# The low parts of gate and up's operands, of sixteen weight units and of products 5 and 7: GpSimd's share of the subtractions given to VectorE

## The chip, the cores and the metric

The kernel runs on one core of a Trainium2 chip. The metric is the device time of one execution in microseconds (us). The engines have queues of their own: TensorE (PE; its weight loads are PEld) does the matrix products, VectorE (DVE) and GpSimd (POOL) element-wise work, ScalarE (ACT) copies, casts and functions, and SyncE (SP) issues the transfers.

## The reference

A decoder of two layers on 1024 tokens of width 1024, in float32. A layer normalises its input and makes one input projection whose columns go to three token mixers, an RWKV-7 recurrence, a dilated window attention and a latent attention. Their outputs are joined, projected and added to the input. Then comes the part that the change touches:

```python
    for l in range(DEPTH):
        ...
        x = x + jnp.concatenate([ya, yb, yc], axis=-1) @ w_out[l]
        h = rms_norm(x, ffn_norm_g[l])
        x = x + (jax.nn.silu(h @ ffn_w_gate[l]) * (h @ ffn_w_up[l])) @ ffn_w_down[l]
    return rms_norm(x, final_norm_g)
```

`D_FF` is 2816, that is 22 columns of 128 in `ffn_w_gate` and `ffn_w_up`.

## The kernel before

All matrices are held as tiles of 128x512, with features on the partitions and half of the tokens (512) along the row. A product of two float32 matrices is made from three matmuls: each operand is split into a high part, its cast to the matmul's type, and a low part, the rest, and `mm3` sums high by high, high by low and low by high in PSUM. A split is one cast on ScalarE (`acopy`, L295, rows named `wh`, `hhi`, `mhi`, `ahi`) and one subtraction of 128x512 on VectorE or GpSimd (`tt`, L301, rows named `wl`, `hlo`, `mlo`, `alo`). Which of the two it is, `split` is told by its caller.

Gate and up are made with Strassen's scheme: the matrix of 8 by 2 blocks of activations and a pair of weight columns give seven products of four blocks each (twelve matmuls) in place of eight. Product 1 takes the weight block a11, 6 takes a21+a22-a11, 7 takes a11-a21, 2 takes a12, 5 takes a21+a22, 4 takes a22 and 3 what is left; the right operands are sums of `hx`, the normalised activations, made by `sums` on VectorE. They are made in the order 1, 6, 7, 2, 5, 4, 3. There are eleven pairs for each of gate and up, so 22 blocks (`Four`) in a layer. Of the first eight of them products 1 and 2 come ahead of all others (`early`), since these need only the first half of the tokens: their sixteen operands are the weight units `("g"...)` and `("u"...)` of `loader`, while all later weight operands are made by `Operands`. A `Four` uses four banks of PSUM. ScalarE copies product 1 out (`u`), and then product 2 may be added to its bank; VectorE adds product 6 to `u`, product 7 to that (`v<-u,gu`), after which product 4 may use 7's bank, and product 5 (`v<-v,gu`), after which product 3 may use 5's. The results of gate and up are multiplied on GpSimd (`v<-v`; one of four on VectorE), VectorE makes the sums that the down product needs from them, splits these seven (`alo`), and they go to DRAM. Down's first eighteen rows of blocks are made by the same scheme from `Operands` in three stages of four blocks each, the last four rows in the plain way.

The order of every engine's queue is fixed when the program is built. Strands of work (generators) are run by a planner (`Flow.run`): it keeps a clock for each engine, prices an operation (`tt`: columns x 1.04 + 65 ns on VectorE, x 2.2 + 65 ns on GpSimd, `F.op`), and takes next the strand that can start first, with a lower `prio` number first among those that could start at the same time. Strands of weights and of adds out of PSUM have 2, operand sums and the splits of activations mostly 3. Nothing is reordered at run time: an instruction at the head of its engine's queue holds up what is behind it. The weights go through a ring of six operand pairs, so that a further one is split only after an earlier one was used.

The operand splits of gate and up (`put`) and those of the mixers' outputs (`mix_split`) ask `sub_eng` for their engine, which names VectorE and GpSimd by turns. The weight units are split on GpSimd; of the products' operands 6, 2 and 4 are split on VectorE, 1, 3, 5 and 7 on GpSimd.

Of the kernel before, what the change touches and what calls it, by code (L numbers as in the profile page):

```python
# [231 lines left out]
def trunk(ctx: ExitStack, tc: tile.TileContext, xT, pos, vec, con, first, w_in, small, uq, uqr, ukv,  # L232
# [60 lines left out]
    def acopy(out, in_):  # L293
        F.op("act", cols(in_) * 0.833 + 80)
        nc.scalar.copy(out=out, in_=in_)  # L295
# [3 lines left out]
    def tt(eng, out, a, b, op):  # L299
        F.op(eng, cols(out) * (1.04 if eng == "dve" else 2.2) + 65)  # L300
        ENG[eng].tensor_tensor(out=out, in0=a, in1=b, op=op)  # L301
# [22 lines left out]
    def dma(out, in_, nbytes):  # L324

        s = F.cur
        start = max(s.at(), F.clock["dma"])
        F.clock["dma"] = start + max(450.0, nbytes / 360.0)
        nc.sync.dma_start(out=out, in_=in_)
        return F.clock["dma"] + 2000  # L330
# [8 lines left out]
    def f32(ap):  # L339
        return ap.bitcast(F32)  # L340
# [22 lines left out]
    def room(level):  # L363

        return lambda: sum(max(n, 0) for lv, n in reserve.items() if lv < level)

    def pages(where, names, dt=F32, keep=0, of=None):

        def taken(n):
            if of in reserve:  # L370
                reserve[of] -= n

        got = yield Need(lambda: [P[w] for w in where], len(names), keep, taken if of else None)
        of = of if of in reserve else None
        out = []
        for n, s in zip(names, got):
            n, d = n if isinstance(n, tuple) else (n, dt)
            t = s.pool.tile([128, HALF], d, tag="hp", name=n)
            owner[id(t)] = (s, t, of)
            out.append(t)  # L380
        return out

    def page(where, name, dt=F32, keep=0, of=None):
        return (yield from pages(where, [name], dt, keep, of))[0]

    def free(*tiles):
        for t in tiles:
            s, _, of = owner.pop(id(t))
            if of is few:
                F.give(few)  # L390
            elif of in reserve:
                reserve[of] += 1
            F.give(s)
# [68 lines left out]
    def sub_eng():  # L462
        flip[0] ^= 1
        return "dve" if flip[0] else "pool"

    def split(src, hi, lo, eng):

        yield "act"
        acopy(hi, src)
        yield eng  # L470
        tt(eng, lo, src, f32(hi), ALU.subtract)
# [5 lines left out]
    def again(k):  # L477
        return k[0] in pairs_dram and k[2] == 1
# [3 lines left out]
    def loader(items):  # L482

        there.update({k: Event() for k, _ in items if k[0] in pairs_dram})

        def keep(k):
            late, soon = room(4), room(1)
            at = k[1][0][1] if k[0] == "S" else k[1]
            return lambda: soon() if k[0] == "in" or at < at_layer[0] else late()

        def own(k):

            rest, ffn = keep(k), k[0] in "gusS"
            return lambda: room(3.2)() if ffn and 3.2 in reserve else rest()

        def parts(k, srcs):

            if k[0] != "S":
                return [(Event(), srcs)]
            n = range(len(k[1]))  # L500
            at = [(g, 0) for g in n] + [(g, b) for g in n for b in (1, 2)] + [(g, 3) for g in n]
            return [(Event(), srcs[g][b], g, b) for g, b in at]

        def pair(k):

            return pairs_dram[k[0]][k[1], k[3], k[4]]

        queue = [(k, [] if again(k) else parts(k, srcs), own(k)) for k, srcs in items]

        def fetch():  # L510
            for k, todo, keep in queue:
                for ev, part, *_ in todo:
                    yield Need([raws])
                    wr = yield from page(["gp"], "wr", keep=keep, of=3.2)
                    w, t = 0, 0.0
                    yield "dma"
                    for a in part:
                        n = a.shape[-1]
                        t = dma(wr[:, w:w + n], a, 512 * n)
                        w += n  # L520
                    F.set(ev, wr, t)

        def raw_free(wr):
            free(wr)
            F.give(raws)

        F.spawn(fetch(), 1)
        for k, todo, keep in queue:
            if again(k):
                yield there[(*k[:2], 0, *k[3:])]  # L530
                yield Need([ring])
                w = yield from pages(["gp"], ["wh", "wl"], F32R, keep, 3.2)
                at = pair(k)
                yield "dma"
                for i in range(2):
                    t = dma(f32(w[i]), at[i], 262144)
                F.set(W[k], w, t)
                continue
            if k[0] == "S":
                gs = []  # L540
                for g, key in enumerate(k[1]):
                    evs = {b: ev for ev, _, g_, b in todo if g_ == g}
                    gs.append(Operands(key, k[2], evs, todo[0][1][0].shape[-1], keep, raw_free))
                for r in k[2]:
                    for g in gs:
                        yield from g.make(r)
                continue
            wr = yield todo[0][0]
            yield Need([ring])
            wh, wl = yield from pages(["gp"], ["wh", "wl"], F32R, keep, 3.2)  # L550
            yield from split(wr, wh, wl, "pool")
            raw_free(wr)
            now = F.cur.at()
            if k[0] in pairs_dram:
                yield "dma"
                for i, w in enumerate((wh, wl)):
                    t = dma(pair(k)[i], f32(w), 262144)
                F.set(there[k], None, t)
            F.set(W[k], (wh, wl), now)

    class Operands:
# [6 lines left out]
        def out(self, r, src, then=None):  # L568
            yield Need([ring])
            wh, wl = yield from pages(["gp"], ["wh", "wl"], F32R, self.keep, 3.2)  # L570
            w = self.w

            def one():
                yield from split(src[:, w], wh[:, w], wl[:, w], "dve" if r in (6, 2, 4) else "pool")
                if then:
                    then(src)
                F.set(W[(*self.key, r)], (wh, wl))

            F.spawn(one(), 2)
# [433 lines left out]
    def layer(l):  # L1013
# [1058 lines left out]
        def ffn():  # L2072
# [50 lines left out]

            def put(src, ev, where_=both, last=True):
                hi, lo = yield from pages(where_, ["hhi", "hlo"], F32R, keep)
                yield from split(src, hi, lo, sub_eng())
                if last:
                    free(src)
                F.set(ev, (hi, lo))

            def first_half(k):
                a = yield hx[0][k]
                F.spawn(put(a, Bg[1][k], last=False), 3)
                a = yield hx[0][k + 4]
                F.spawn(put(a, Bg[2][k], last=False), 3)

            def sums(k):
                b12 = yield hx[1][k]
                b22 = yield hx[1][k + 4]
                b11, b21 = hx[0][k].val, hx[0][k + 4].val  # L2140
                t1, t2 = yield from pages(both, ["t1", "t2"], keep=keep)
                yield "dve"
                tt("dve", t1, b12, b11, ALU.subtract)
                yield "dve"
                tt("dve", t2, b22, t1, ALU.subtract)
                F.spawn(put(t2, Bg[6][k], last=False), 2)
                yield "dve"
                tt("dve", b12, b22, b12, ALU.subtract)
                F.spawn(put(b12, Bg[7][k]), 2)
                F.spawn(put(t1, Bg[5][k]), 3)  # L2150
                yield Bg[1][k]
                free(b11)
                yield Bg[2][k]
                yield "dve"
                tt("dve", b21, b21, t2, ALU.subtract)
                F.spawn(put(b21, Bg[4][k]), 3)
                F.spawn(put(b22, Bg[3][k]), 3)
                yield Bg[6][k]
                free(t2)
# [5 lines left out]
            for hf in range(2):  # L2165
# [4 lines left out]
                for c in range(KD):  # L2170
# [4 lines left out]
                    for n_, k in enumerate(KORDER):  # L2175
# [4 lines left out]
                        w = yield W["wo", l, hf, c, k // 4]  # L2180
# [354 lines left out]
        def weights():  # L2535
            yield w_start
            yield from loader(items)
# [24 lines left out]
    def first_weights():  # L2562
        F.cur.t = 1500.0
        yield from loader(in_items(0))
# [139 lines left out]
```

## Time and profile before

| what | value |
|---|---|
| median of 3 runs | 2620.64 us (2617.64 to 2624.98) |
| the profiled execution's own time | 2621.2 us |
| its span, first to last instruction | 2619.4 us |
| TensorE busy | 2533.5 us, 97% |
| VectorE busy | 1747.4 us, 67% |
| ScalarE busy | 1135.3 us, 43% |
| GpSimd busy | 1154.9 us, 44% |
| mean granted TensorE clock | 0.983 |

Times in the profile are counted from the first instruction. Gate and up begin at about 655 us in layer 0 and at about 1949 us in layer 1. A busy share is an average over stages that differ; what TensorE waits for has to be read stage by stage.

### The profile page before, as it was taken

How to read it: one execution, taken by the hardware profiler on the slowest of the kernel's cores; microseconds unless marked ns; L12 is line 12 of the kernel's file. 1: busy time of each engine (PE TensorE's matmuls, PEld its weight loads, DVE VectorE, ACT ScalarE, POOL GpSimd, SP SyncE). 2: the span in 40 equal slices, each digit the busy share in tenths (PEclk: the TensorE clock that was granted, in tenths of full speed). 3: DMA queues.
4: the chain of work that ended last, by engine and by line, in shares of the span. 5: the costliest groups of instructions: out<-in, count | busy, mean ns of one | idle time of the engine just before them, and what ended most of it. 6: DMA issues, size and time to landing. Idle time of an engine off the chain costs nothing. (4 is left out here: it accounts for less than half of the span.)

```text
span 2619.4 us, 38866 instructions
## 1 busy us (share of the span) xinstructions
PE 2533.5 (97%) x13112; PEld 2030.1 (78%) x13112; DVE 1747.4 (67%) x3415; ACT 1135.3 (43%) x2313; POOL 1154.9 (44%) x914
## 2 busy tenths in 40 slices
PE   7899999999899999999999999999998999999998
PEld 6678765888688888888878787568887888888887
DVE  6856677764987657566567376677458877665566
ACT  6542475663434334323354326557544334333221
POOL 3513231366645444455553123214655544444660
PEclk9999998999999999999999999999999999999999
DMA  7662321135255434896485241201461545449851
GB/s 265 234 211 88 118 64 29 56 115 199 99 176 194 140 134 161 307 316 229 166 290 194 93 171 36 63 25 53 168 198 60 197 165 177 147 136 351 291 196 65
DMA packets 235800, 417.55 MB, mean 159 GB/s; under 512 B 27600, under 2 KB 45264, under 8 KB 235472
## 3 DMA queue, kind: packets, MB, share of 16 engines
q1 hardware_dynamic: 235600, 415.07, 46.6%
q8 instruction: 103, 1.69, 0.3%
q14 instruction: 97, 0.79, 0.1%
HBM read 269.60 MB, written 141.69 MB: 157 GB/s over the span
## 5 line engine op out<-in xcount | busy, mean ns | idle before, releaser
L301 POOL TENSOR_TENSOR wl<-wr,wh 128x512 fp32r<-128x512 f32 (+1 forms) x304 | 436.5, 1448 | 387.0 <-ACT wh L295 310.2
L266 PE MATMUL gu<-hhi,wh 128*128 128x512 f32 x1232 | 483.7, 393 | 22.8 <-ACT u L295 16.5
L266 PE MATMUL gu<-hlo,wh 128*128 128x512 f32 x1232 | 481.1, 390 | 0.0
L266 PE MATMUL gu<-hhi,wl 128*128 128x512 f32 x1232 | 481.0, 390 | 0.0
L266 PEld LDWEIGHTS gu<-hhi,wh 128*128 128x128 f32 x1232 | 232.3, 189 | 79.6 <-ACT u L295 18.1
L295 ACT CAST wh<-wr 128x512 fp32r<-128x512 f32 (+1 forms) x424 | 244.4, 593 | 77.3 <-POOL wl L301 21.4
L266 PEld LDWEIGHTS gu<-hhi,wl 128*128 128x128 f32 x1232 | 232.3, 189 | 48.6
L266 PEld LDWEIGHTS gu<-hlo,wh 128*128 128x128 f32 x1232 | 232.4, 189 | 47.7
L301 POOL TENSOR_TENSOR wl<-s,wh 128x512 fp32r<-128x512 f32 (+1 forms) x136 | 181.5, 1342 | 197.1 <-ACT wh L295 142.8
L266 PE MATMUL dn<-bhi,wh 128*128 128x512 f32 (+1 forms) x664 | 252.0, 380 | 0.0
L266 PE MATMUL dn<-blo,wh 128*128 128x512 f32 (+1 forms) x664 | 251.5, 379 | 0.0
L266 PE MATMUL dn<-bhi,wl 128*128 128x512 f32 (+1 forms) x664 | 251.2, 379 | 0.0
L266 PE MATMUL inp<-hhi,wh 128*128 128x512 f32 x512 | 213.9, 418 | 11.4 <-ACT wh L295 11.4
L295 ACT CAST wh<-s 128x512 fp32r<-128x512 f32 (+1 forms) x204 | 116.8, 581 | 247.0 <-DVE s L301 199.7
L266 PE MATMUL inp<-hhi,wl 128*128 128x512 f32 x512 | 205.6, 401 | 5.2 <-POOL wl L301 5.2
L266 PE MATMUL inp<-hlo,wh 128*128 128x512 f32 x512 | 204.9, 400 | 1.2 <-DVE hlo L310 1.2
L301 DVE TENSOR_TENSOR x<-x,dn 128x512 f32<-128x512 f32 (+1 forms) x160 | 104.6, 657 | 109.3 <-PE dn L266 86.7
L301 DVE TENSOR_TENSOR v<-u,gu 128x512 f32<-128x512 f32 x132 | 90.1, 682 | 126.4 <-PE gu L266 126.2
L301 POOL TENSOR_TENSOR v<-v 128x512 f32<-128x512 f32 x66 | 98.0, 1488 | 134.3 <-DVE v L301 133.4
L291 ACT ACTIVATE P<-P,mx 128x512 f32<-128x512 f32 (+1 forms) x192 | 117.5, 613 | 63.9 <-DVE mx L857 42.5
L266 PEld LDWEIGHTS dn<-bhi,wh 128*128 128x128 f32 x664 | 124.9, 188 | 23.5
L266 PEld LDWEIGHTS dn<-bhi,wl 128*128 128x128 f32 x664 | 124.9, 188 | 23.4
(319 smaller groups left out, 5403.6 us busy)
## 6 DMA issues: line engine op xcount, KB each, us to landing
act_dram<-ahi SPq DMA_DIRECT2D x142, 256.0 KB
act_dram<-alo SPq DMA_DIRECT2D x142, 256.0 KB
bhi<-act_dram SPq DMA_DIRECT2D x142, 256.0 KB
blo<-act_dram SPq DMA_DIRECT2D x142, 256.0 KB
wr<-in_w_gate_dram SPq DMA_DIRECT2D x104, 256.0 KB
wr<-in_w_up_dram SPq DMA_DIRECT2D x104, 256.0 KB
wr<-in_w_in_dram SPq DMA_DIRECT2D x72, 256.0 KB
pairs_in<-wh SPq DMA_DIRECT2D x72, 256.0 KB
```

The source lines that it names most:

```text
L266: nc.tensor.matmul(out=out, lhsT=lhsT, rhs=rhs, start=start, stop=stop, **kw)
L291: nc.scalar.activation(out=out, in_=in_, func=func, **kw)
L295: nc.scalar.copy(out=out, in_=in_)
L301: ENG[eng].tensor_tensor(out=out, in0=a, in1=b, op=op)
```

## The change

Three places in which the low part was made by GpSimd, wholly or by turns, name VectorE: the sixteen weight units of gate and up, the weight operands of products 5 and 7 (of gate, up and down), and all operands of gate and up. Weight units of the input and output projections and of the last part of down, and products 1 and 3, stay on GpSimd. `sub_eng` isn't called by `put` any more, so `mix_split` and the norms have its turns to themselves.

```diff
@@ loader @@
             wh, wl = yield from pages(["gp"], ["wh", "wl"], F32R, keep, 3.2)
-            yield from split(wr, wh, wl, "pool")
+            yield from split(wr, wh, wl, "dve" if k[0] in "gu" else "pool")
             raw_free(wr)
@@ Operands.out @@
             def one():
-                yield from split(src[:, w], wh[:, w], wl[:, w], "dve" if r in (6, 2, 4) else "pool")
+                yield from split(src[:, w], wh[:, w], wl[:, w], "dve" if r in (6, 2, 4, 5, 7) else "pool")
                 if then:
@@ ffn, put @@
                 hi, lo = yield from pages(where_, ["hhi", "hlo"], F32R, keep)
-                yield from split(src, hi, lo, sub_eng())
+                yield from split(src, hi, lo, "dve")
                 if last:
```

## Rows read from the trace of the kernel before

**Rows 1.** The page, span and part 1: busy us, share of the span, instructions.

```profile
span 2619.4 us, 38866 instructions
...
PE 2533.5 (97%) x13112; PEld 2030.1 (78%) x13112; DVE 1747.4 (67%) x3415; ACT 1135.3 (43%) x2313; POOL 1154.9 (44%) x914
```

**Rows 2.** Windows: length, busy us (instructions) of PE, PEld, DVE, ACT, POOL; clock, DMA.

```profile
655.00:720.50 65.50, 55.33 (x243) 44.92 (x242) 59.82 (x67) 31.14 (x55) 41.60 (x27) 0.95 0.30 98
...
1179.00:1244.50 65.50, 65.50 (x290) 54.26 (x289) 43.30 (x64) 20.65 (x44) 38.66 (x32) 1.00 0.68 229
```

**Rows 3.** TensorE's waits over the span: us in total, times, longest.

```profile
PE gu L266 <- ACT u L295: 16.5, 4, 6.0
...
PE gu L266 <- DVE v L301: 3.2, 12, 1.3
PE gu L266 <- ACT ahi L295: 3.1, 4, 0.9
```

**Rows 4.** TensorE's timeline, three places: start, us, instruction, [idle before, releaser].

```profile
686.04 0.39 PE L266 MATMUL gu<-hhi,wl 128*128 128x512 f32 x1
688.72 0.50 PE L266 MATMUL gu<-hhi,wh 128*128 128x512 f32 x1 [2.29 <-ACT u L295]
...
699.52 0.39 PE L266 MATMUL gu<-hhi,wl 128*128 128x512 f32 x1
705.87 0.80 PE L266 MATMUL gu<-hhi,wh 128*128 128x512 f32 x1 [5.96 <-ACT u L295]
...
1999.63 0.79 PE L266 MATMUL gu<-hhi,wh 128*128 128x512 f32 x1 [5.93 <-ACT u L295]
```

**Rows 5.** Windows around the long wait, columns as in rows 2 (clock third from last).

```profile
692.00:700.00 8.00, 7.91 (x35) 6.20 (x34) 8.00 (x7) 4.93 (x9) 8.00 (x5) 1.00 0.31 98
...
706.00:712.00 6.00, 6.00 (x21) 4.85 (x22) 5.41 (x6) 2.97 (x6) 4.82 (x4) 0.77 0.14 50
...
2000.00:2006.00 6.00, 6.00 (x15) 4.62 (x15) 5.45 (x6) 2.41 (x6) 4.36 (x3) 0.52 0.01 5
```

**Rows 6.** Timelines of VectorE, GpSimd and ScalarE, 655 to 715 us.

```profile
665.36 5.36 DVE L310 SCALAR_TENSOR_TENSOR hx<-x,vecs,ssum 128x512 f32<-128x512 f32 x8 [0.74 <-PE ssum L276]
...
695.57 5.17 DVE L301 TENSOR_TENSOR hlo<-hx,hhi 128x512 fp32r<-128x512 f32 x3
...
704.00 0.68 DVE L301 TENSOR_TENSOR s<-s,wr 128x512 f32<-128x512 f32 x1
...
698.46 5.07 POOL L301 TENSOR_TENSOR hlo<-hx,hhi 128x512 fp32r<-128x512 f32 x3
...
686.44 1.22 ACT L295 CAST hhi<-hx 128x512 fp32r<-128x512 f32 x2 [1.62 <-DVE hx L301]
...
688.09 0.58 ACT L295 COPY u<-gu 128x512 f32<-128x512 f32 x1
...
704.71 0.62 ACT L295 CAST wh<-s 128x512 fp32r<-128x512 f32 x1 [5.01 <-DVE s L301]
705.24 0.58 ACT L295 COPY u<-gu 128x512 f32<-128x512 f32 x1
```

**Rows 7.** Windows of layer 0's start of gate and up, columns as in rows 2.

```profile
665.00:706.00 41.00, 32.75 (x145) 26.50 (x143) 40.55 (x40) 21.50 (x38) 26.15 (x16) 0.95 0.21 69
706.00:815.00 109.00, 107.45 (x464) 87.75 (x465) 92.18 (x118) 42.39 (x76) 52.59 (x35) 0.99 0.50 169
```

**Rows 8.** VectorE's waits in 665 to 706 us: all that there are.

```profile
DVE hx L310 <- PE ssum L276: 0.7, 1, 0.7
```

**Rows 9.** Timelines of VectorE, GpSimd and TensorE in the steady stage, around 914 us.

```profile
914.59 1.28 DVE L301 TENSOR_TENSOR alo<-v,ahi 128x512 fp32r<-128x512 f32 x2
...
917.00 0.68 DVE L301 TENSOR_TENSOR v<-v,gu 128x512 f32<-128x512 f32 x1
...
913.82 4.41 POOL L301 TENSOR_TENSOR wl<-wr,wh 128x512 fp32r<-128x512 f32 x1 [5.11 <-ACT wh L295]
...
917.82 0.47 PE L266 MATMUL gu<-hhi,wh 128*128 128x512 f32 x1 [0.17 <-DVE v L301]
```

## The prediction

> **What bounds the kernel now.** The page comes first: TensorE is busy for 2533.5 of 2619.4 us, VectorE for 1747.4, GpSimd for 1154.9 [rows 1]. A reader should take from it that a gain can come only from time in which TensorE doesn't get its next matmul, some 86 us, and that the question is how much of this the edited splits cause. The windows tell where it is. In a slice where nothing is late TensorE shows 65.50 of 65.50 us and 290 matmuls, 0.226 us each; in the slice in which gate and up begin it shows 55.33 and 243 [rows 2]. The list of TensorE's waits names what it waited for there: the copy `u` of ScalarE, 16.5 us in four waits over the whole span, so two in each layer, and in small pieces `v` of VectorE (3.2 us) and `ahi` (3.1 us) [rows 3]. TensorE's timeline gives the two long waits of layer 0: from 686.04 to 688.72, and from 699.52 to 705.87; the later one of layer 1 ends at 1999.63 and is as long [rows 4]. After it the granted clock falls as well: 0.77 in 706 to 712 us and 0.52 in 2000 to 2006, so part of both is at 1.2 GHz, while after the shorter wait it stays at 1.00 [rows 5].
>
> Why does `u` come late, a copy out of PSUM of 0.58 us? ScalarE's timeline shows it behind others in ScalarE's queue: the one at 688.09 stands behind casts of `hx` for which ScalarE waited 1.62 us, the one at 705.24 behind the cast of `s`, for which it waited 5.01 us, and that operand is a sum of VectorE made at 704.00 [rows 6]. So VectorE is late. In 665 to 706 it is busy 40.55 of 41 us with only 40 operations [rows 7], and all that it waited there is 0.7 us at the start [rows 8]. It works without a pause, and slowly: three rests `hlo` take 5.17 us, over 1.7 each, beside GpSimd's three at 1.7 each [rows 6]. Where VectorE runs through undisturbed, two rests take 1.28 us together and a single operation 0.68, so one follows another every 0.60 us [rows 9]. In this stretch the two engines take turns: one operation of each in about 1.72 us.
>
> **The change part by part.** Nothing is computed twice and nothing added: a subtraction of 128x512 goes from one queue to the other. Per layer there are 14 of the 28 operand rests (each second one so far), 16 weight units, and products 5 and 7 of 22 gate and up blocks and 12 down blocks, 68: together 98, so 196 in all. No DMA and no wait on a DMA queue is moved. What changes with it is order: the program's queues are written by a planner that prices a VectorE subtraction at about 0.60 us and a GpSimd one at 1.19, each as if the other engine weren't there. The first price is the undisturbed row of VectorE; what the contended rows cost isn't in it. With the rests on VectorE the planned queue should thus be nearer to the time that it really takes.
>
> *The start of gate and up.* GpSimd has 16 operations in 665 to 706, and VectorE 40 [rows 7]. All of these 16 are units or operand rests and move. VectorE then has 56. Eight are the normalised `hx`, which read PSUM and are no slower today (eight in 5.36 us [rows 6]); the other 48 at 0.60 make 28.8: 34.1 us in all, from 665.4 to 699.5. At 0.68 each, the isolated price, it would be 37.9 us, to 703.3. Today the same work ends at about 704.7 for the sum that matters.
>
> What TensorE can win there, in layer 0: the waits of 2.29 and 5.96 us, and 0.16 more for each, since a matmul's row is 0.39 long and the pitch 0.23: 8.57 us [rows 4]. The lower clock in 706 to 712 costs 6 x 0.23 = 1.4 us, in 2000 to 2006 6 x 0.48 = 2.9 us [rows 5]. Layer 1 repeats the waits, so both layers have 2 x 8.57 + 4.3 = 21.4 us.
>
> What may be left of it: without the first wait TensorE asks for the second `u` at 699.75 - 2.45 = 697.3. If the sum of `s` stays at the end of VectorE's 56 operations, `u` is done at 699.5 + 1.1 (cast and copy) = 700.6, a rest of 3.3 us; by the isolated price at 704.4, 7.1 us, which is the whole wait again. If the planner brings this sum forward (sums of weights go ahead of the operand sums in its ranking) nothing is left. I take 1.5 us for each layer, nearer to the lower end, since the row with two back to back gives 0.60 and not 0.68: 21.4 - 3.0 = 18.4 us. A wait of that size left the clock at 1.00 [rows 5], so its part goes with the wait.
>
> *Steady gate and up.* In 706 to 815, where the first eight blocks make five products each, VectorE is busy 92.18 of 109 us in 118 operations, 0.78 each, and GpSimd has 35 [rows 7]. Some 17 of those move: 17 x 0.60 = 10 us more for VectorE, against contention of (0.78 - 0.65) x 118 = 15 us over 35 operations, 0.44 each, so 7.5 us less. VectorE ends at some 95 of 109 us: fuller, not full. The cover is this room of 14 us; where it lacks, see the second rival. I take nothing, with both ends kept: the small waits for `v` and `ahi` all gone would be 6.3 us of idle and some 2.5 of pitch, 9 us; the loss is the second rival's.
>
> *Down.* TensorE was at 65.50 of 65.50 beside 43.30 of VectorE in such a slice [rows 2]; twelve blocks bring two rests each, 24 x 0.60 = 14 us spread over some 200 us per layer. Nothing: it lies behind matmuls that don't wait.
>
> The sum: 2621.2 us is the profiled execution's own time, 1.8 more than its span and 0.6 above the median of 2620.64. 2621.2 - 18.4 = 2602.8, which against the median is 2602.
>
> **A rule and its row.** At 913.82 a GpSimd rest took 4.41 us while VectorE went on at 0.60 [rows 9]: there GpSimd paid for the overlap and VectorE nothing. The Trainium skill (SBUF — State Buffer, "Who interferes with whom") says that a VectorE instruction with two SBUF inputs and a GpSimd instruction that reads SBUF exclude each other for the whole instruction, and that the order of issue decides who is blocked. The trace agrees with that second half by the 4.41 us, and with exclusion by the 1.7 us. This speaks against the change wherever VectorE runs without a pause, since a rest on GpSimd is then free for VectorE and costs it 0.60 after the move. By the row of 1.7 us the steady stage costs nothing and the sum stays 2602; by this rule alone each moved rest in a burst is a loss, and the sum is that of the second rival.
>
> **The rivals.** First, VectorE's one queue bounds the start: 3.3 to 7.1 us of the second wait stay in each layer. For it: VectorE is already full there, and the operations grow from 40 to 56. Against: 56 at 0.60 are fewer microseconds than 40 contended ones. The gain is then 21.4 - 6.6 = 14.8 at best and, with the whole wait and the clock's fall back, 2 x 2.45 = 4.9 us: between 2606 and 2616, about 2613.
>
> Second, it gets slower by one mechanism: product 3 takes over the bank of product 5 and can start only when VectorE has added that into `v`. At 917.00 this add stands behind a run of rests of activations, and the matmul after it waits 0.17 us [rows 9]: no room is left. Each block boundary between up and the next gate has such a burst, 11 a layer. A moved rest of product 5 or 7 that is put in front of that add delays product 3 by its 0.60 us in full. One a burst: 22 x 0.60 = 13 us; two: 26 us, 2602 + 26 = 2628; two in every one of the 44 blocks, 53 us, 2655. It decides from two a burst on. Against it: the planner ranks that add above the rests of activations, so that a moved rest should push one of those back, not the add; and a GpSimd rest that now holds VectorE up in the burst, at the 0.44 us worked out above, goes with the move.
>
> Third, the move does what it says and the planner's new order gives the time back: each later choice, layer 1's attention too, is made from other clocks, and a chain of small operations can come out some microseconds longer. The price is that of the gain: 2621 within 8 us. For it speaks that the order is decided at build time over the whole span; against it, that the operations of those other stages don't change and that nothing in the profile gives their shift a direction. That rests go to GpSimd again by another path is excluded: the diff names all three.
>
> **How the numbers follow.** The forecast has 0.60, 2593 to 2612, with 2602 in it. The first rival 0.15, about 2613, of which 0.06 is faster by over 0.3% (7.9 us, below 2612.8) and 0.09 not; 0.3% is also about what a measurement here tells from no change. The second 0.15, 0.11 beyond 2628 and 0.04 with one rest a burst, near 2615 to 2620. The third 0.10: 0.07 within, 0.01 faster, 0.02 slower. Faster 0.67, same 0.20, slower 0.13. The range goes from 2593 (18.4 us and the 9 us of small waits) to 2619, which takes in the first rival and leaves out the second's worse half.
>
> **What would show it.** After the change there should be no GpSimd rest at all between the start of gate and up and its first product 3, VectorE's operations there some 0.6 us apart with some 56 of them in 35 us, no wait of TensorE for `u` over 2 us, and a granted clock of 1.00 through that stretch in both layers. VectorE's busy time over the span should rise by less than 196 x 0.60 = 118 us, since contention goes. I am wrong if `u` still ends waits of 5 us (first rival), if waits for `v` of a microsecond come at each boundary (second), or if those waits are gone and others of the same sum stand elsewhere (third).

## The result and the profile after

The changed kernel takes 2596.07 us (2587.61 to 2599.44) against 2622.81 (2617.64 to 2625.68) in the runs of both: a ratio of 0.989, interval 0.9872 to 0.9909, that is 24 to 34 us. The forecast was 2602 and faster.

The page after the change, span and part 1, as in [rows 1]:

```profile
span 2597.7 us, 38718 instructions
...
PE 2536.6 (98%) x13112; PEld 2035.6 (78%) x13112; DVE 1785.0 (69%) x3611; ACT 1134.1 (44%) x2313; POOL 883.5 (34%) x718
```

VectorE has exactly the 196 operations more (3415 to 3611) and GpSimd 196 fewer. VectorE's busy time rose by 37.6 us only, 0.19 for each operation, while GpSimd's fell by 271. At 0.60 us each the moved operations alone would be 118 us, so something like 80 us of VectorE's busy time went elsewhere; the experiments show that it was time spent held up by GpSimd.

The windows of the changed kernel, columns as in [rows 2]: the 41 us from the first normalised operands on (it is the stretch of [rows 7], which lies 9 us later here), the stage of the early blocks, gate and up in both layers from first to last matmul, and what comes before them:

```profile
673.80:714.80 41.00, 41.00 (x184) 33.96 (x183) 40.35 (x66) 25.69 (x46) 3.05 (x1) 1.00 0.27 88
716.00:825.00 109.00, 108.56 (x479) 89.31 (x478) 91.66 (x138) 41.34 (x74) 32.63 (x21) 1.00 0.54 181
665.60:1090.00 424.40, 422.55 (x1862) 347.61 (x1861) 320.56 (x492) 170.09 (x309) 106.84 (x70) 1.00 0.50 169
1942.40:2366.90 424.50, 422.65 (x1863) 347.67 (x1862) 321.34 (x494) 170.12 (x309) 106.84 (x70) 1.00 0.49 170
...
0.00:571.60 571.60, 543.35 (x3261) 416.60 (x3262) 389.07 (x1018) 303.40 (x662) 193.91 (x189) 0.95 0.37 124
```

The same windows of the kernel before:

```profile
655.50:1094.50 439.00, 425.13 (x1863) 348.23 (x1862) 319.36 (x429) 170.86 (x310) 209.04 (x136) 0.99 0.48 164
1949.20:2388.70 439.50, 426.76 (x1863) 349.43 (x1862) 317.40 (x429) 171.17 (x310) 212.03 (x136) 0.99 0.48 164
...
0.00:561.50 561.50, 531.14 (x3262) 406.75 (x3262) 390.69 (x1018) 303.55 (x662) 193.08 (x189) 0.97 0.38 127
```

Gate and up take 14.6 us less in layer 0 and 15.0 less in layer 1, with 63 VectorE operations more in about the same busy time (319.36 and 320.56 us). The first stretch, before the output projection, has the same instructions on all engines in both kernels and took 10.1 us longer in this profiled execution, at a mean granted clock of 0.95 against 0.97. So the spans differ by only 21.7 us, and the profiled execution of the changed kernel is the slowest of its four. From here on stages are compared, not spans.

At the start VectorE is as full as before (40.35 of 41 us), but makes 66 operations in it where it made 40 [rows 7]: 0.61 each. TensorE is busy for 41.00 of 41.00 at a clock of 1.00. The one GpSimd operation there is a weight rest of product 3; the prediction wanted none before the first product 3, which can't be, since product 3's own weights are still split on GpSimd. TensorE's waits in gate and up of layer 0, first after and then before:

```profile
PE gu L266 <- DVE v L301: 1.4, 6, 0.2
PE gu L266 <- ACT ahi L295: 0.4, 1, 0.4
```

```profile
PE gu L266 <- ACT u L295: 8.2, 2, 6.0
PE gu L266 <- DVE v L301: 2.1, 6, 1.3
PE ssum L276 <- DVE ry L310: 1.9, 1, 1.9
PE gu L266 <- ACT ahi L295: 1.5, 2, 0.9
```

Both waits for `u` are gone, and so is one that the prediction had not counted: `ssum <- ry`, where TensorE waited for the last step of the norm's root.

### The profile page after: what moved, and what is told of

The parts are those of the page before. It is cut to its first block, busy times and chain, and to the rows that moved or that the text cites. A ratio compares the mean times of both kernels' runs of the same rounds, so it can differ in the third digit from the quotient of the medians.

```text
span 2597.7 us, 38718 instructions
## 1 busy us (share of the span) xinstructions
PE 2536.6 (98%) x13112; PEld 2035.6 (78%) x13112; DVE 1785.0 (69%) x3611; ACT 1134.1 (44%) x2313; POOL 883.5 (34%) x718
## 5 line engine op out<-in xcount | busy, mean ns | idle before, releaser
L301 POOL TENSOR_TENSOR wl<-wr,wh 128x512 fp32r<-128x512 f32 (+1 forms) x204 | 279.9, 1384 | 189.4 <-ACT wh L295 157.0
L301 POOL TENSOR_TENSOR wl<-s,wh 128x512 fp32r<-128x512 f32 (+1 forms) x68 | 94.3, 1395 | 452.9 <-ACT wh L295 371.7
L266 PE MATMUL inp<-hhi,wh 128*128 128x512 f32 x512 | 215.0, 420 | 10.1 <-ACT wh L295 10.1
L301 POOL TENSOR_TENSOR v<-v 128x512 f32<-128x512 f32 x66 | 105.7, 1602 | 208.6 <-DVE v L301 183.1
L301 DVE TENSOR_TENSOR wl<-wr,wh 128x512 fp32r<-128x512 f32 (+1 forms) x220 | 156.8, 717 | 18.3 <-ACT wh L295 17.9
L301 POOL TENSOR_TENSOR x<-x,u 128x512 f32<-128x512 f32 x72 | 103.9, 1473 | 153.6 <-DVE u L301 136.6
```

The lines of the kernel that those rows point to most:

```text
L266: nc.tensor.matmul(out=out, lhsT=lhsT, rhs=rhs, start=start, stop=stop, **kw)
```

## The experiments

Times are medians of 5 to 12 executions; the kernel before, run beside them, had medians of 2621.35, 2621.86 and 2623.26 us in the three sets.

**The three parts, each alone.** The diff's hunks one at a time. First the operands:

```diff
-                yield from split(src, hi, lo, sub_eng())
+                yield from split(src, hi, lo, "dve")
```

> Only the operand rests of gate and up go to VectorE (14 a layer); units and products 5 and 7 stay on GpSimd. Contention theory: 9 of GpSimd's 16 operations in the first 41 us of gate and up go, so about 9/16 of what that stretch gives back, some 25 us over both layers, is won: 14 us, near 2608; GpSimd still has its weight rests beside VectorE's operations of 1.7 us. Rival, that the planner's new order makes the gain: no relation to the share, anything from 2596 to 2625.

2610.09 us, ratio 0.9959 (0.9946 to 0.9972): near the 2608 of the contention theory, but within the rival's wide range too, so the time alone doesn't part them. Gate and up took 432.9 us in layer 0; of the long wait 1.1 us is left, and the norm's 1.9 us stay, since the weight units were still with GpSimd there:

```profile
PE gu L266 <- DVE v L301: 2.9, 7, 1.9
PE ssum L276 <- DVE ry L310: 1.9, 1, 1.9
...
PE gu L266 <- ACT u L295: 1.1, 1, 1.1
```

Then the weight units alone:

```diff
-            yield from split(wr, wh, wl, "pool")
+            yield from split(wr, wh, wl, "dve" if k[0] in "gu" else "pool")
```

> Only the sixteen weight units go to VectorE; operand rests by turns, products 5 and 7 on GpSimd. Contention theory: 7 of 16 operations go and with them the long tiny operations of the norm before it: about 11 + 4 us, near 2607. Rival (new order): no relation to the share, 2596 to 2625.

2634.71 us, ratio 1.0055 (1.0036 to 1.0074): slower, by 14 us, where the contention theory had forecast 14 faster. The forecast by shares fell. Gate and up took 445.7 us in layer 0 and 445.6 in layer 1, 6.7 and 6.1 more than before, so nearly all of the loss is there. TensorE's waits in layer 0 show two effects:

```profile
PE gu L266 <- DVE v L301: 8.0, 6, 1.3
PE gu L266 <- ACT u L295: 5.0, 2, 3.8
PE gu L266 <- ACT ahi L295: 4.0, 2, 3.2
```

The norm's wait is gone and those for `u` are shorter (5.0 for 8.2), as the theory wants. But the waits for `v` went from 2.1 to 8.0 us, six times 1.3, in the later part of gate and up, where no weight unit is left. (Those for `ahi` grew too, from 1.5 to 4.0; what made them longer wasn't traced.) A burst there, on VectorE, GpSimd and TensorE, shows what lengthens the waits for `v`:

```profile
924.30 2.38 DVE L301 TENSOR_TENSOR alo<-v,ahi 128x512 fp32r<-128x512 f32 x2
...
929.02 0.67 DVE L301 TENSOR_TENSOR v<-v,gu 128x512 f32<-128x512 f32 x1
...
924.19 1.35 POOL L301 TENSOR_TENSOR wl<-wr,wh 128x512 fp32r<-128x512 f32 x1 [4.57 <-ACT wh L295]
...
929.84 0.47 PE L266 MATMUL gu<-hhi,wh 128*128 128x512 f32 x1 [1.35 <-DVE v L301]
```

It is the burst of [rows 9] with one difference. There GpSimd's rest came while VectorE was running through and took 4.41 us, at no cost to VectorE. Here it starts at 924.19, 0.11 us ahead of the first `alo`, and takes 1.35; the two `alo` take 2.38 us in place of 1.28. VectorE is 1.1 us later at `v<-v,gu`, and TensorE's wait grew by 1.35 - 0.17 = 1.18. In the new plan the cast that this rest waits for stands one place earlier on ScalarE. The Trainium skill (SBUF — State Buffer, "Who interferes with whom") says that the order of issue decides which of the two is held up; these two bursts, 4.41 us on the one side and 1.1 on the other, agree that either can be. The 4.41 us are more than that order gives, which the prediction didn't say: GpSimd's row there begins at 913.82, and the two `alo` from 914.59 on, which begin later, went ahead of it all the same [rows 9]. No run here shows why.

Products 5 and 7 alone:

```diff
-                yield from split(src[:, w], wh[:, w], wl[:, w], "dve" if r in (6, 2, 4) else "pool")
+                yield from split(src[:, w], wh[:, w], wl[:, w], "dve" if r in (6, 2, 4, 5, 7) else "pool")
```

> Only products 5 and 7 of the weights go to VectorE. In the start of gate and up nothing of them runs, so both long waits for the copy u stay (2.3 and 6 us a layer). Contention theory: at most the small waits of later pairs go, 2 to 6 us, near 2618. The rival of the prediction by which bursts get longer: 13 us slower with one more rest a burst, near 2635. New order alone: within 2615 to 2625.

2619.48 us, ratio 0.9994 (0.9979 to 1.0009): no change, and no sign of the slower rival. The `u` waits stayed (9.3 us in layer 0, two). Together the three parts bring 27 us, singly 11, -14 and 1.6: they don't add up. Two reasons fit the traces, without being parted here: what each leaves on GpSimd goes on holding up VectorE, and each makes a plan of its own.

**Engines against order.** To part the two, the subtraction was priced on one engine's clock and issued on another. In the first cross everything is planned as before and the moved rests are issued on VectorE:

```diff
+        if plan:
+            yield plan
+            F.op(plan, cols(lo) * (1.04 if plan == "dve" else 2.2) + 65)
+            ENG[eng].tensor_tensor(out=lo, in0=src, in1=f32(hi), op=ALU.subtract)
+            return
...
-                yield from split(src, hi, lo, sub_eng())
+                yield from split(src, hi, lo, "dve", sub_eng())
```

> All three parts issued on VectorE, but planned at the price and on the clock of GpSimd as before, so that the order of TensorE, ScalarE and of everything that isn't moved is that of the kernel before. Contention theory: most of the gain comes without a new order, at least 20 of some 27 us, near 2600. Rival (new order makes the gain): the long waits for u stay, since u stands behind the same casts, and the time is 2615 to 2622.

2605.00 us, ratio 0.9936 (0.9919 to 0.9954): 17 us of the 27, less than the 20 that were expected, and well outside the rival's 2615 to 2622. The old order was kept nearly: by the traces three matmuls, two ScalarE instructions and some eight of VectorE's unmoved operations stand elsewhere in each layer. The start of gate and up lost its waits but for one of 1.2 us, and in the bursts those for `v` grew from 0.17 to 0.78. The window of gate and up in layer 0, and the waits in it:

```profile
660.30:1089.40 429.10, 423.14 (x1861) 347.17 (x1861) 323.49 (x495) 170.48 (x310) 103.91 (x70) 1.00 0.49 168
...
PE gu L266 <- DVE v L301: 4.7, 6, 0.8
PE gu L266 <- ACT wh L295: 1.2, 1, 1.2
```

The burst's rows, VectorE and TensorE, in this run (L473 is the line added to `split`, so a moved rest) and then in the changed kernel:

```profile
908.28 1.28 DVE L301 TENSOR_TENSOR alo<-v,ahi 128x512 fp32r<-128x512 f32 x2
909.49 0.68 DVE L473 TENSOR_TENSOR wl<-wr,wh 128x512 fp32r<-128x512 f32 x1
910.09 1.28 DVE L301 TENSOR_TENSOR alo<-t,ahi 128x512 fp32r<-128x512 f32 x2
911.29 0.68 DVE L301 TENSOR_TENSOR v<-v,gu 128x512 f32<-128x512 f32 x1
...
912.12 0.47 PE L266 MATMUL gu<-hhi,wh 128*128 128x512 f32 x1 [0.78 <-DVE v L301]
```

```profile
911.65 0.68 DVE L301 TENSOR_TENSOR wl<-wr,wh 128x512 fp32r<-128x512 f32 x1
912.25 0.68 DVE L301 TENSOR_TENSOR alo<-v,ahi 128x512 fp32r<-128x512 f32 x1
912.85 0.68 DVE L301 TENSOR_TENSOR alo<-t,ahi 128x512 fp32r<-128x512 f32 x1
913.45 0.68 DVE L301 TENSOR_TENSOR v<-v,gu 128x512 f32<-128x512 f32 x1
...
914.65 0.68 DVE L301 TENSOR_TENSOR alo<-t,ahi 128x512 fp32r<-128x512 f32 x1
...
914.28 0.47 PE L266 MATMUL gu<-hhi,wh 128*128 128x512 f32 x1 [0.25 <-DVE v L301]
```

One moved rest (`wl`, at 909.49) ahead of the add makes TensorE's wait 0.61 us longer: the second rival's mechanism at its price. In the changed kernel the rest stands there too, but the planner has put one `alo` behind the add for it, so the wait is 0.25.

The other cross has the changed kernel's plan, with the rests issued where they were before.

```diff
-                yield from split(src, hi, lo, sub_eng())
+                yield from split(src, hi, lo, sub_eng2(), "dve")
```

> The other cross: planned as the changed kernel, all moved rests priced on VectorE's clock, but issued on the engines of before (units and products 5 and 7 on GpSimd, operands by turns). Contention theory: VectorE is contended again, so the waits for u are back and the time is 2612 to 2630. Rival (new order makes the gain): 2596 to 2605.

2632.17 us, ratio 1.0035 (1.0019 to 1.0050). TensorE's matmuls stand exactly in the order of the changed kernel, and this order with the old engines is slower than the kernel before. The waits are back, but not where they were expected: those for `u` are 0.6 us, those for `v` 10.4. Layer 0:

```profile
663.20:1106.80 443.60, 427.88 (x1862) 350.40 (x1861) 318.43 (x429) 169.28 (x309) 195.31 (x136) 0.99 0.47 162
...
PE gu L266 <- DVE v L301: 10.4, 8, 5.5
...
PE gu L266 <- ACT u L295: 0.6, 1, 0.6
```

From the windows from first to last matmul of gate and up, layer 0, in us:

| | rests issued as before | rests issued on VectorE |
|---|---|---|
| planned as before | 439.0 | 429.1 |
| planned as changed | 443.6 | 424.4 |

In this layer the engines are worth 9.9 us with the old plan and 19.2 with the new; the plan is worth 4.7 us, and only with the new engines. Layer 1 gives 11.0, 19.1 and 4.0.

**Contention put back.** GpSimd makes each moved rest a second time into a tile that nothing reads, and the planner doesn't know of it. The tile needs the room of one page, so a run of the changed kernel with 78 pages stands beside it.

```diff
+    idle = fix.tile([128, HALF], F32, name="idle")
...
         tt(eng, lo, src, f32(hi), ALU.subtract)
+        if twin:
+            n = cols(lo)
+            nc.gpsimd.tensor_tensor(out=idle[:, :n], in0=src, in1=f32(hi), op=ALU.subtract)
```

> The changed kernel, and GpSimd makes each moved rest once more into a tile that nobody reads, unpriced by the planner, so that GpSimd's old work stands beside VectorE's new. One page fewer in the big pool (78), as in the run beside it. Contention theory: VectorE's operations at the start of gate and up take 1.7 us again, now 56 of them, and the time goes back to before or beyond it: 2620 to 2660. Rival (the gain lies in the order or in GpSimd's chain being off the path): nobody waits for the copies, so 2596 to 2602.

> The changed kernel with one page fewer in the big pool (78 for 79), the measure for the run with the doubled rests. All theories: as the changed kernel, 2590 to 2602.

With the copies 2652.69 us (ratio 1.0127, 1.0104 to 1.0149), without 2581.58 (0.9853, 0.9823 to 0.9883). Windows of gate and up in layer 0, first with the copies, with 63 us at the start and TensorE's longest waits, then without:

```profile
661.70:1119.60 457.90, 432.19 (x1862) 352.17 (x1861) 362.53 (x493) 170.40 (x309) 225.27 (x137) 0.97 0.46 158
...
672.00:735.00 63.00, 47.65 (x201) 37.99 (x199) 62.78 (x71) 26.72 (x47) 38.16 (x22) 0.91 0.16 52
...
PE gu L266 <- DVE v L301: 13.9, 8, 12.1
```

```profile
659.30:1083.80 424.50, 422.65 (x1862) 347.64 (x1861) 320.94 (x493) 170.02 (x309) 106.77 (x70) 1.00 0.50 170
```

The same 493 VectorE operations take 362.53 us for 320.94, and the stage 33.4 us longer. By the traces every engine's other instructions stand in the same order in both runs, and nothing computed depends on a copy; only the release of buffers does. ScalarE waited for such a release for 1.1 us in this stage. In the stretch behind it, where it waited 12.5 us for them, the run with the copies took 748.6 us for 747.6, so the release isn't what costs. At the start VectorE needs 62.78 us for 71 operations: 0.88 each and not the 1.7 that was expected, since the copies don't run beside all of them. TensorE once waits 12.1 us for `v`, where the kernel before waited for `u`. So the contention by itself makes VectorE late and TensorE wait; which tile TensorE waits for differs with the plan.

The run without copies was meant as a measure and came out 14 us below the changed kernel, outside what was expected. Its gate and up take the same time (424.5 and 424.4). Of the 17.1 us between the two profiled executions 10.8 lie between gate and up of layer 0 and the output projection of layer 1 (747.6 us for 758.4, at a clock of 0.99 for 0.98), and the other 6.3 ahead of gate and up:

```profile
1083.80:1831.40 747.60, 734.78 (x4211) 579.31 (x4209) 504.33 (x1176) 349.38 (x765) 288.47 (x256) 0.99 0.46 154
```

**Further versions.** All weights of the products on VectorE, products 1 and 3 too:

```diff
-                yield from split(src[:, w], wh[:, w], wl[:, w], "dve" if r in (6, 2, 4, 5, 7) else "pool")
+                yield from split(src[:, w], wh[:, w], wl[:, w], "dve")
```

> The changed kernel with products 1 and 3 on VectorE as well, so that no weight of gate, up and down's products is split on GpSimd. Contention theory: two of GpSimd's rests stretch two VectorE operations by 1.1 us each in every burst after an up block; moved they cost 1.2 in all, so the waits for v of 0.25 us and for ahi go: 2 to 6 us faster than the changed kernel, near 2592. Rival (VectorE's queue becomes the bound, 66 more operations a layer): waits for v of 1 us at each boundary, 2605 or more.

2589.19 us, ratio 0.9877 (0.9856 to 0.9898). Against the changed kernel gate and up won 1.2 us a layer: the waits for `v` are gone, as expected; those for `ahi`, which were to go too, grew from 0.4 to 2.2 us. The intervals of the two kernels overlap.

```profile
661.70:1084.90 423.20, 420.96 (x1862) 348.13 (x1861) 329.70 (x532) 171.84 (x309) 48.79 (x32) 1.00 0.50 170
```

This version and the kernel before, each with 78 pages:

```diff
-    G_BUFS, L_BUFS, NRAW, NW = 79, 19, 3, 6
+    G_BUFS, L_BUFS, NRAW, NW = 78, 19, 3, 6
```

> All weights of gate, up and down's products and all operands on VectorE, with 78 pages. If what 78 pages gave came from a shorter plan of layer 1's mixers, and what products 1 and 3 gave from gate and up, both add: some 2 us below the changed kernel with 78 pages in gate and up, near 2580. If the mixers' plan falls out by chance, that part can be lost: near 2590.

> The kernel before with 78 pages and nothing else. If the page count itself shortens the time between gate and up of layer 0 and the output projection of layer 1, some 11 us are won here too: near 2611. If that was one chance plan, the time stays near 2621. Gate and up stay near 439 us a layer in either case, since the engines of the rests are those of before.

2589.98 us (0.9854, 0.9831 to 0.9877) and 2619.96 (0.9981, 0.9966 to 0.9997). The stretch after gate and up of layer 0 was 747.3 and 752.5 us, with 79 pages 762.6 and 760.7. So 78 pages shorten that stretch in all three kernels, but the medians don't follow it. Of the 8 us that it gives the kernel before, its median keeps 3. And this version has the shorter gate and up (423.2 us) and the short stretch both, but its ratio is only equal to that of the changed kernel with 78 pages, and its median 8 us above it. The 2.6 us that its gate and up win over both layers are less than these intervals tell apart. By the ratios the two with 78 pages and the new engines are the fastest here, and their intervals overlap that of the changed kernel.

## Why the prediction was right

*VectorE is late, and late by contention.* Shown. The doubled rests bring waits back with the order unchanged, and the first cross removes those for `u` with the old order all but kept.

*The start's account.* Foreseen were the two waits for `u`, 8.57 us a layer, and the lost clock, 1.4 and 2.9 us; both went whole. The rest of 1.5 us a layer didn't come: after the change these two copies `u` wait for TensorE's own matmuls, with nothing late ahead of them on ScalarE. The sum `s` on VectorE and the two copies:

```profile
697.49 0.69 DVE L301 TENSOR_TENSOR s<-s,wr 128x512 f32<-128x512 f32 x1
...
689.09 0.59 ACT L295 COPY u<-gu 128x512 f32<-128x512 f32 x1 [0.17 <-PE gu L266]
...
699.97 0.59 ACT L295 COPY u<-gu 128x512 f32<-128x512 f32 x1 [1.13 <-PE gu L266]
```

The sum `s` that the second `u` had stood behind was made at 697.49, before the last operand sums, and no longer at the end of VectorE's operations, as the planner's ranking suggested.

*What was mis-sized.* Forecast were 18.4 us; gate and up give 29.6 by the traces, and the medians 26.7. The missing 11 us are: the 3.0 set aside for a rest; the wait for the norm, 1.92 + 0.16 us a layer, so 4.2 in all, which the account left out although GpSimd's weight units run beside it; and the small waits for `v` and `ahi`, taken as nothing: 2.1 + 1.5 us before and 1.4 + 0.4 after in layer 0. These and their pitch come to 2 us there, to less in layer 1. The sum is 10 us of the 11; the last one stays open.

*Steady gate and up.* Forecast was VectorE at some 95 of 109 us there; it is 91.66, with 20 operations more (138 for 118) and 0.5 us less busy time. The contention that went away paid for all the added work, and by this count the estimate of 0.44 us for each GpSimd operation was too low: 12 us of new work at 0.60 and the 0.5 us less, over 14 GpSimd operations fewer (21 for 35), are 0.9 us each, in two windows that don't hold quite the same work.

*The rivals.* The first, VectorE's queue as the bound of the start, fell: it is full, yet early enough. The second is real in its mechanism and price (0.61 us for one rest), and is seen where the order stays as it was; in the changed kernel the planner moves an `alo` instead. It comes six times a layer, by the waits for `v`, and not in the 11 bursts that the prediction counted. The third, the new order as such, is no loss here: with the old engines it costs 4.6 us a layer, with the new ones it gives 4.7. Its other half, that stages which nobody touched come out otherwise, holds: the stretch after gate and up of layer 0 varied from 747 to 763 us between these kernels. Most of that goes with the page count, 747 to 753 us with 78 and 758 to 763 with 79; what of the rest is the plan and what the granted clock stays open.

## What to carry to other kernels

Before an operation is given to an idle GpSimd, see in the trace what VectorE's operations beside it take: here 1.7 us for 0.68, so that a rest of 1.29 us on GpSimd could cost VectorE more than making it itself, and GpSimd's share of 44% looked free and wasn't. The page's busy share hides this, since the time held up counts as busy: 63 operations more fitted into the same 320 us. Parts of such a change need to be tried together; one of these three is a loss alone, where its new plan let a GpSimd rest begin 0.11 us ahead of VectorE's burst.

## What the runs showed of the hardware

Small operations are held up as well. In the norm's root before the change, beside GpSimd's weight rests, operations of 128x4 took over a microsecond:

```profile
659.75 1.29 DVE L306 TENSOR_SCALAR rh<-rh 128x4 f32<-128x4 f32 x1
660.95 0.15 DVE L301 TENSOR_TENSOR rt<-ry 128x4 f32<-128x4 f32 x1
661.14 1.14 DVE L301 TENSOR_TENSOR rt<-rt,rh 128x4 f32<-128x4 f32 x1
...
663.50 1.12 DVE L310 SCALAR_TENSOR_TENSOR ry<-rt,ry 128x4 f32<-128x4 f32 x1
...
659.72 2.54 POOL L301 TENSOR_TENSOR wl<-wr,wh 128x512 fp32r<-128x512 f32 x2 [0.62 <-PE ssum L266]
663.34 1.26 POOL L301 TENSOR_TENSOR wl<-wr,wh 128x512 fp32r<-128x512 f32 x1 [1.08 <-issue]
```

After the change each takes 0.16 us. The last of them is the `ry` that TensorE waited 1.92 us for. The second and third end within 0.02 us of a GpSimd rest's end (662.28 and 662.26, 664.62 and 664.60), so an operation that is held up lasts until GpSimd's is over, however short it is itself: the Trainium skill (SBUF — State Buffer, "Who interferes with whom") gives that as a lock held for the whole instruction, and these ends agree. `rt<-ry` passed in 0.15 us; it begins at 660.95, where one GpSimd rest gives way to the next.
